# A turn of products by column lanes and the neighbouring full turn, multiplied column block by column block

## The chip, the core and the metric

The kernel runs on one core of a Trainium2 chip. The metric is the device time of one execution in microseconds. TensorE multiplies, VectorE (DVE), ScalarE (ACT) and GpSimd (POOL) compute beside it, SyncE (SP), ACT and POOL issue DMAs, and 16 DMA engines move the data.

## The reference

One layer of an encoder on 256 positions of width 2048: modulated norms, a conv group and an attention group, an output projection, and then a retrieval over 16384 experts (`peer_ffn`). The change lies in the last sum of that retrieval. For each token, 8 heads choose 16 experts each; cut to what matters:

```python
expert = i1 * 128 + i2                       # 8 heads x 16 experts a token
a   = einsum('td,tnd->tn', h, u_tab[ids])    # u_tab: 16384 x 2048
act = gelu(a) * gate
out = einsum('tn,tnd->td', act, v_tab[ids])  # v_tab: 16384 x 2048
y   = rms_norm(x + gt_f * out, g_final)
```

## The kernel before, in words

The retrieval is dense in its first half: for each of the 128 blocks of 128 experts, `ru` (1 MB of `peer_u`) is loaded, split in a high and a low part (L239, L240), and multiplied with the tokens (`pu`, lines 257 to 263). Gate times GELU of these scores, zero where a token did not choose the expert, is written to memory (`actd`, one row of 256 tokens per expert).

The second half is sorted. While the scores are still made, POOL sorts the experts by which of eight groups of 32 tokens use them, so that they fill 109 blocks of 128 experts (`ORDER` is their order). A block needs, for each half `tt` of 128 tokens, all four groups, or a pair of neighbouring ones, or a single one. `plan()` turns this, as plain Python while the program is built, into a list of 89 **turns**:

- 48 *full* turns: one block, one half of the tokens, 128 columns of weights;
- 21 *pair* turns: two blocks side by side, each with 64 columns;
- 20 *single* turns: four blocks side by side, each with 32 columns.

In pairs and singles the blocks sit in column lanes of TensorE (`tile_position`), and their matmuls go at the same time. The list mixes the kinds as blocks come up; the last four turns are full ones (`DEFER`).

For a block, POOL gathers 128 rows of `peer_v` (L1355, `fetch_raw`, 128x2048 in float32, into a tile named `rv`, `rvd`, `rvg`, `early` or `A`) and the matching rows of `actd` (L1366, `fetch_m`, into `mc` or `mcs`). A lane multiplies these two as they are, in float32; each such product is two weight loads and two matmuls in the records. A full turn uses parts: `split_to` (L246 on ACT, L247 on DVE) makes high and low parts of the rows (`hwhi`/`hwlo`, the two halves of `hboth`, and near the end `hx`) and of the weights (`mhl`), and three products are summed, high by high, low by high, high by low. The parts have three slots to begin with (`wide`); up to 15 blocks are fetched ahead (`AHEAD`).

`product` (L1444) is one product of one column block: 512 of the 2048 columns of the result (`d4` from 0 to 3). The eight tiles `po` (two halves of tokens by four column blocks) hold the sum in PSUM through the whole stage. TensorE runs the products in the order in which they are written (`keep`); gathers, splits and products wait for each other by semaphores.

The loop that writes them goes over the turns with index `i`. Ahead of each group of turns it frees slots and tiles of turns below `i`, writes the gathers and splits that are due, and then the products:

```python
for d4s in ((range(4),) if len(group) == 1 and group[0][0][2] == "full" else [(d4,) for d4 in range(4)]):
    for k, p in enumerate(group):
        for t in range(3):
            for n, at, kind in p:
                if t == 0 or kind == "full":
                    r, m = split[n][t] if kind == "full" else (raws[n], ms[n])
                    for d4 in d4s:
                        product(r, m, at, SIZE[kind], d4, ...)
i += len(group)
```

So a full turn by itself takes its three products in turn, each through the four column blocks. A turn by lanes goes by column block, with all its lanes in each. Before the change a group is one turn, but for the last three turns, which are one group and go by column block. When the products are done, `finish` scales the sum, adds it to `x`, normalises and writes the result.

Of the kernel before, what the change touches and what calls it, by code (L numbers as in the profile page):

```python
# [10 lines left out]
F32R = mybir.dt.float32r  # L11
# [156 lines left out]
def hybrid_block_kernel(  # L168
# [25 lines left out]
    cst = ctx.enter_context(tc.tile_pool(name="cst", bufs=1))  # L194
# [93 lines left out]
    with tc.tile_pool(name="pre", bufs=1) as pre:  # L288
# [482 lines left out]
        for q in range(4):  # L771
# [4 lines left out]
            for u in range(4 * NG0):  # L776
                g, n = divmod(u, 4)
                i = NG0 * q + g
# [567 lines left out]
    turns, need = plan()  # L1346
# [104 lines left out]
        for _ in range(4 * (1 - k)):  # L1451
            fetch_m(m_free.pop(0)[-1])
    wide = [(-1, [wp.tile([128, 2048], F32R, tag=t, name=f"h{t}{k}") for t in ("whi", "wlo")]) for k in range(2)]
    both = cst.tile([128, 2, 2048], F32R, tag="T1", name="hboth")
    wide.append((-1, [both[:, 0], both[:, 1]]))
    mhl = cst.tile([128, 8, 256], F32R, tag="T3a", name="mhl")
    narrow = [(-1, k) for k in range(4)]
    mcs = cst.tile([128, 8, 256], F32, tag="T3b", name="mcs")
# [40 lines left out]
    first_last = len(turns) - len(DEFER)  # L1499

    i = 0
    while i < len(turns):
        group = turns[i:i + 1] if i < len(turns) - 3 else turns[i:]
        now = max(x[0] for p in group for x in p)
        for x in [x for x in live if x[0] < i]:
            live.remove(x)
# [194 lines left out]
```

## Time and profile before

| what | value |
|---|---|
| median of three runs | 1691.31 us (1676.72 to 1833.54) |
| the profiled execution | 1675.07 us, span 1673.3 us |
| mean granted TensorE clock | 0.980 |
| first matmuls of `po` in the trace | about 1321 us |
| first turn by lanes | 1334 us |
| last matmul of `po` | ends about 1660 us |
| DMA over the whole span | 502.55 MB, mean 300 GB/s |

Times in the trace are microseconds from the start of the span. A row of the timeline has the start, the length from the first start to the last end, the engine (PE is TensorE's matmuls, PEld its weight loads), the line, the operation, result and operands, the shapes (rows*columns of weights, then the moving operand), the count, and in brackets the idle time ahead of it with what ended it. A row of waits has who waited, for whom, the total in us, how often, and the longest.

### The profile page before, as it was taken

Reading aid. Unit: us, or ns where it says so; the run is one execution under the profiler, and the core shown is the slowest. Engines: PE = TensorE matmul, PEld = TensorE weight load, DVE = VectorE, ACT = ScalarE, POOL = GpSimd, SP = SyncE. Lnnn points to the kernel's source line nnn. Section 1 sums busy time; section 2 is a strip of 40 time slices with the busy share of each in tenths; the row PEclk is TensorE's granted clock in tenths of the full one; section 3 lists DMA queues with packets and bytes.
Section 4 is the critical chain, followed back from the end, with each engine's and each line's share of the span. In section 5 each row is a group of like instructions: output and inputs, shape, how many; then the busy total and the mean of one; then the engine's idle time right before and its main releaser. Section 6 shows DMA issues by size and latency. Waiting matters only on the chain.

```text
span 1673.3 us, 30110 instructions
## 1 busy us (share of the span) xinstructions
PE 1595.5 (95%) x12776; PEld 1387.4 (83%) x12780; DVE 1124.2 (67%) x1610; ACT 707.6 (42%) x901; POOL 430.4 (26%) x356
## 2 busy tenths in 40 slices
PE   3999999999999999999999999999999989899996
PEld 2879899999899999999999999999999746433443
DVE  5778778867678889998997875575765425222316
ACT  3225557544544446655663334343343324222213
POOL 0000000000000000000000007888873466565651
PEclk9999999999999999999999999999999999999998
DMA  9996998889665556656668789999999889999995
GB/s 395 425 410 233 351 337 328 310 303 335 239 233 172 187 203 202 243 175 239 224 235 285 249 272 270 302 363 361 335 348 397 299 347 346 360 379 375 378 345 226
DMA packets 115725, 502.55 MB, mean 300 GB/s; under 512 B 13392, under 2 KB 55888, under 8 KB 60288
## 3 DMA queue, kind: packets, MB, share of 16 engines
q1 hardware_dynamic: 44640, 319.79, 51.6%
q0 software_dynamic: 25184, 129.25, 20.2%
q10 hardware_dynamic: 45760, 51.51, 9.6%
q8 instruction: 102, 1.67, 0.4%
q14 instruction: 39, 0.32, 0.1%
HBM read 462.57 MB, written 37.94 MB: 299 GB/s over the span
## 4 chain that ended last, share of the span: by engine, by line
PE 84%; DVE 7%; issue 4%; DMA 3%; ACT 1%; SPq 0%; DVEq 0%; ACTq 0%
PE po L1444 19%; PE pu L257 11%; PE pu L258 11%; PE pu L263 11%; PE pin L748 4%; DMA ru<-in_peer_u_dram 3%; PE pwin L257 2%; PE pwin L258 2%; PE pwin L263 2%; DVE lu L240 2%; PE pwout L257 2%; PE pwout L258 2%; PE pwout L263 2%; PE pq L258 2%; PE pq L257 2%
## 5 line engine op out<-in xcount | busy, mean ns | idle before, releaser
L257 PE MATMUL pu<-h2hi,hu 128*128 128x256 f32 x2048 | 481.0, 280 | 2.8 <-ACT hu L239 2.8
L239 ACT ACTIVATE hu<-ru 128x2048 fp32r<-128x2048 f32 x128 | 245.8, 1920 | 393.7 <-PE pu L258 286.2
L240 DVE TENSOR_TENSOR lu<-ru,hu 128x2048 fp32r<-128x2048 f32 x128 | 293.1, 2290 | 167.3 <-ACT hu L239 125.4
L257 PEld LDWEIGHTS pu<-h2hi,hu 128*128 128x128 f32 x2048 | 385.8, 188 | 3.6 <-ACT hu L239 3.2
L263 PE MATMUL pu<-h2hi,lu 128*128 128x256 f32 x2048 | 253.9, 276 | 0.9 <-DVE lu L240 0.9
L258 PE MATMUL pu<-h2loT3b,hu 128*128 128x256 f32 x1024 | 247.5, 278 | 0.0
L1288 POOL DMA_INDIRECT permd<-work x126 | 206.6, 1639 | 148.8 <-DVE work L1284 110.7
L263 PEld LDWEIGHTS pu<-h2hi,lu 128*128 128x128 f32 x2048 | 242.0, 188 | 1.1 <-DVE lu L240 1.1
L258 PE MATMUL pu<-h2loT3a,hu 128*128 128x256 f32 x1024 | 241.2, 278 | 0.0
L1320 POOL DMA_DIRECT2D gg<-gd x3 | 4.2, 1398 | 882.1 <-DMA permd<-pad 882.1
L258 PEld LDWEIGHTS pu<-h2loT3b,hu 128*128 128x128 f32 x1024 | 192.9, 188 | 0.2 <-issue 0.2
L258 PEld LDWEIGHTS pu<-h2loT3a,hu 128*128 128x128 f32 x1024 | 193.0, 188 | 0.0
L1444 PE MATMUL po<-rv,mc 128*32 128x512 f32 (+1 forms) x336 | 94.5, 601 | 3.1 <-issue 2.6
L1355 POOL DMA_INDIRECT rv<-in_peer_v_dram,perm_idx x66 | 67.9, 1029 | 96.3 <-ACT A L1386 29.9
L1444 PE MATMUL po<-hwhi,mhl 128*128 128x512 f32 x272 | 79.5, 413 | 12.2 <-issue 12.1
L240 DVE TENSOR_TENSOR lwin<-rwin,hwin 128x2048 fp32r<-128x2048 f32 x33 | 75.5, 2289 | 21.7 <-ACT hwin L239 20.3
L239 ACT ACTIVATE hwin<-rwin 128x2048 fp32r<-128x2048 f32 x33 | 63.1, 1912 | 57.2 <-PE pin L748 31.8
L1444 PE MATMUL po<-rv,mcs 128*32 128x512 f32 (+1 forms) x312 | 86.2, 628 | 1.0 <-issue 0.7
L1444 PEld LDWEIGHTS po<-hwhi,mhl 128*128 128x128 f32 x272 | 51.7, 195 | 38.0 <-issue 25.5
L257 PE MATMUL pwin<-hhi,hwin 128*128 128x256 f32 x336 | 81.0, 285 | 0.0
L258 PE MATMUL pwin<-hlo,hwin 128*128 128x256 f32 x336 | 78.7, 278 | 0.0
L284 DVE SCALAR_TENSOR_TENSOR acc<-ada,cact,acc 128x2048 f32<-128x2048 f32 x30 | 70.4, 2347 | 10.1 <-DMA ada<-in_w_ada_dram 9.7
(594 smaller groups left out, 3173.5 us busy)
## 6 DMA issues: line engine op xcount, KB each, us to landing
ru<-in_peer_u_dram SPq DMA_DIRECT2D x128, 1024.0 KB
ada<-in_w_ada_dram SPq DMA_DIRECT2D x96, 1024.0 KB
rwin<-in_w_in_dram SPq DMA_DIRECT2D x33, 1024.0 KB
rwout<-in_w_out_dram SPq DMA_DIRECT2D x16, 1024.0 KB
rwq<-in_w_q_dram SPq DMA_DIRECT2D x16, 1024.0 KB
gd<-stage ACTq DMA_DIRECT2D x16, 1024.0 KB
actd<-A ACTq DMA_DIRECT2D x14, 1024.0 KB
gg<-gd ACTq DMA_DIRECT2D x13, 1024.0 KB
```

Of the source, the lines that this page charges most:

```text
L239: S.activation(hi, raw, AF.Copy)
L240: lo_op = V.tensor_tensor(lo, raw, hi.bitcast(F32), ALU.subtract)
L257: PE.matmul(dst, lhsT=whi[:, sl], rhs=rhi[:, c], start=(c == sets[0][0]), stop=False)
L258: PE.matmul(dst, lhsT=whi[:, sl], rhs=rlo[:, c], start=False, stop=False)
L263: PE.matmul(dst, lhsT=wlo[:, sl], rhs=rhi[:, c], start=False, stop=(c == cs[-1] and cs == last))
L284: op = V.scalar_tensor_tensor(acc, raw, cact[:, k:k + 1], acc, ALU.mult, ALU.add)
L748: PE.matmul(dst, lhsT=wt[:, (4 * n + j) * 128:(4 * n + j + 1) * 128], rhs=ht[:, 4 * q + j], start=start, stop=stop, skip_group_check=True)
L1288: put_one = nc.gpsimd.indirect_dma_start(permd[:, :], bass.IndirectOffsetOnAxis(ap=place[:, i:i + 1], axis=0), ids[:, i:i + 1], None)
L1320: keep((S if 1 < k < NG - 1 else nc.gpsimd).dma_start(gg, gd[:, :, k * ABLK:(k + 1) * ABLK, :].rearrange("tb p i t -> p tb i t")))
L1355: keep(nc.gpsimd.indirect_dma_start(raw, None, v_rows, index(ORDER[len(raws)])))
L1444: keep(PE.matmul(po[tt * 4 + d4][row:row + size], lhsT=m[:, at * size:(at + 1) * size], rhs=raw[:, d4 * 512:(d4 + 1) * 512], start=start, ...
```

## The change

Where exactly one of two neighbouring turns is full, and both lie ahead of the last four turns (`first_last`), they now form one group. A group of two goes by column block: for each of the four, the first turn's products and then the second's. A tile's Python name is changed as well, since `both` is now that condition.

```diff
-    both = cst.tile([128, 2, 2048], F32R, tag="T1", name="hboth")
-    wide.append((-1, [both[:, 0], both[:, 1]]))
+    hboth = cst.tile([128, 2, 2048], F32R, tag="T1", name="hboth")
+    wide.append((-1, [hboth[:, 0], hboth[:, 1]]))
...
     while i < len(turns):
-        group = turns[i:i + 1] if i < len(turns) - 3 else turns[i:]
+        both = i + 1 < first_last and (turns[i][0][2] == "full") != (turns[i + 1][0][2] == "full")
+        group = turns[i:i + 1 + both] if i < len(turns) - 3 else turns[i:]
```

The list of turns gives 28 such groups: 10 of a full turn and a pair, 4 of a pair and a full turn, 7 of a full turn and singles, 7 of singles and a full turn. On TensorE, between matmuls of L1444 next to each other in the program, 22 go from 128 columns to fewer and 22 back before the change, and 106 each way after it; 9 go between 64 and 32 columns in both.

TensorE where the first full turn and the first pair meet, before (`hboth` are the parts of the full turn's block; `po` 14769 to 14772 are the four column blocks of the first half of the tokens, 14773 to 14776 those of the second):

```order
L1444 MATMUL po_14769<-hboth,mhl 128x512
L1444 MATMUL po_14770<-hboth,mhl 128x512
L1444 MATMUL po_14771<-hboth,mhl 128x512
L1444 MATMUL po_14772<-hboth,mhl 128x512
L1444 MATMUL po_14773<-rv_13991,mc_14648 64x512
L1444 MATMUL po_14773<-early,mc_14647 64x512
L1444 MATMUL po_14774<-rv_13991,mc_14648 64x512
L1444 MATMUL po_14774<-early,mc_14647 64x512
```

These are the last four of the full turn's twelve rows and the first four of the pair's eight. The same place after the change, the whole of both turns:

```order
L1444 MATMUL po_14769<-hboth,mhl 128x512 x3
L1444 MATMUL po_14773<-rv_13991,mc_14648 64x512
L1444 MATMUL po_14773<-early,mc_14647 64x512
L1444 MATMUL po_14770<-hboth,mhl 128x512 x3
L1444 MATMUL po_14774<-rv_13991,mc_14648 64x512
L1444 MATMUL po_14774<-early,mc_14647 64x512
L1444 MATMUL po_14771<-hboth,mhl 128x512 x3
L1444 MATMUL po_14775<-rv_13991,mc_14648 64x512
L1444 MATMUL po_14775<-early,mc_14647 64x512
L1444 MATMUL po_14772<-hboth,mhl 128x512 x3
L1444 MATMUL po_14776<-rv_13991,mc_14648 64x512
L1444 MATMUL po_14776<-early,mc_14647 64x512
```

The full turn's three products of a column block now stand together, and the pair's of the same block behind them; the kind of matmul changes seven times where it changed once.

TensorE a little later, where four singles and the next full turn meet, before, from the singles' last column block on:

```order
L1444 MATMUL po_14772<-early,mc_14647 32x512
L1444 MATMUL po_14772<-rv_14110,mc_14648 32x512
L1444 MATMUL po_14772<-rv_14224,mc_14649 32x512
L1444 MATMUL po_14776<-early,mc_14647 32x512
L1444 MATMUL po_14769<-hwhi_14789,mhl 128x512
L1444 MATMUL po_14770<-hwhi_14789,mhl 128x512
L1444 MATMUL po_14771<-hwhi_14789,mhl 128x512
L1444 MATMUL po_14772<-hwhi_14789,mhl 128x512
```

And after, from the singles' first column block on:

```order
L1444 MATMUL po_14769<-early,mc_14647 32x512
L1444 MATMUL po_14769<-rv_14110,mc_14648 32x512
L1444 MATMUL po_14769<-rv_14224,mc_14649 32x512
L1444 MATMUL po_14773<-early,mc_14647 32x512
L1444 MATMUL po_14769<-hwhi_14789,mhl 128x512
L1444 MATMUL po_14769<-hwlo_14790,mhl 128x512
L1444 MATMUL po_14769<-hwhi_14789,mhl 128x512
L1444 MATMUL po_14770<-early,mc_14647 32x512
L1444 MATMUL po_14770<-rv_14110,mc_14648 32x512
L1444 MATMUL po_14770<-rv_14224,mc_14649 32x512
L1444 MATMUL po_14774<-early,mc_14647 32x512
```

Here the full turn's first matmul moves from behind all sixteen products of the singles to behind four of them, and the singles' last products move behind three quarters of the full turn.

POOL has the same 109 gathers by L1355 in both programs, block by block in the same order; which tile a block lands in differs, since groups give their tiles back two turns at a time. A stretch of its queue before:

```order
L1366 DMA mc_14647<-actd,ident 128x128
L1355 DMA early<-in_peer_v_dram,perm_idx 128x2048
L1366 DMA mcs<-actd,ident 128x128
L1355 DMA rvd_14779<-in_peer_v_dram,perm_idx 128x2048
L1366 DMA mcs<-actd,ident 128x128
L1355 DMA rv_14110<-in_peer_v_dram,perm_idx 128x2048
```

And the same stretch after:

```order
L1366 DMA mcs<-actd,ident 128x128
L1355 DMA early<-in_peer_v_dram,perm_idx 128x2048
L1366 DMA mc_14647<-actd,ident 128x128
L1355 DMA rv_14110<-in_peer_v_dram,perm_idx 128x2048
L1366 DMA mc_14648<-actd,ident 128x128
L1355 DMA rv_14224<-in_peer_v_dram,perm_idx 128x2048
```

The gathers are the same blocks in the same order; `rvd` and `mcs`, which stood here before, are taken by other blocks now. ACT and DVE have as many instructions as before; a few splits stand some places apart, and read other tiles.

## The prediction

> **What bounds the kernel now.** I read the page's head and its chain first, then the windows of the last stage, who waits there, and last the timeline of TensorE.
>
> ```profile
> PE 1595.5 (95%) x12776; PEld 1387.4 (83%) x12780; DVE 1124.2 (67%) x1610; ACT 707.6 (42%) x901; POOL 430.4 (26%) x356
> PE 84%; DVE 7%; issue 4%; DMA 3%; ACT 1%; SPq 0%; DVEq 0%; ACTq 0%
> ```
>
> ```profile
> 1334.00:1660.00 326.00, 303.45 (x1529) 151.50 (x1528) 106.24 (x195) 88.95 (x186) 187.66 (x194) 0.95 0.90 353
> 1407.00:1445.00 38.00, 38.00 (x197) 22.66 (x194) 13.50 (x24) 11.62 (x24) 25.15 (x25) 1.00 0.91 349
> 1572.00:1583.00 11.00, 11.00 (x49) 7.34 (x49) 2.87 (x5) 2.50 (x5) 8.49 (x9) 1.00 1.01 408
> ```
>
> From the page's head (busy time, share of the span, instructions) and its chain line: TensorE carries the chain of work that ended last. The window rows (length; busy time of PE, PEld, DVE, ACT, POOL; granted clock; DMA share; GB/s) say the same of the last stage: from the first turn by lanes, at 1334, to the last matmul, at 1660, TensorE is busy for 303 of 326 us. DMA is the close second: 0.90 of the stretch, 353 GB/s.
>
> Who waits for whom between 1334 and 1648:
>
> ```profile
> PEld po L1444 <- issue: 146.8, 344, 2.6
> PEld po L1444 <- DMA A<-in_peer_v_dram,perm_idx: 0.9, 1, 0.9
> PEld po L1444 <- ACT mhl L246: 1.7, 2, 0.8
> POOL rv L1355 <- PE po L1444: 21.7, 15, 4.0
> POOL rv L1355 <- DVE hwlo L247: 16.7, 3, 6.5
> ```
>
> TensorE's waits for gathered rows or for a split are about 1 us each. POOL, which issues the gathers, waits for TensorE's buffers and for the splits, and those wait for TensorE's slots. So gathers run ahead of the products, and the order of products sets the stage. "Issue" is time that no releaser explains.
>
> The price of the products, from turns that run undisturbed. A turn by four lanes of 32 columns, two full turns, and the next lanes:
>
> ```profile
> 1391.00 0.59 PE L1444 MATMUL po<-rvd,mcs 128*32 128x512 f32 x1
> ...
> 1391.43 0.59 PE L1444 MATMUL po<-rvd,mcs 128*32 128x512 f32 x1
> ...
> 1391.97 3.03 PE L1444 MATMUL po<-hboth,mhl 128*128 128x512 f32 x12
> 1394.84 1.10 PE L1444 MATMUL po<-hwhi,mhl 128*128 128x512 f32 x4
> 1395.78 1.07 PE L1444 MATMUL po<-hwlo,mhl 128*128 128x512 f32 x4
> 1396.69 1.08 PE L1444 MATMUL po<-hwhi,mhl 128*128 128x512 f32 x4
> ...
> 1397.71 0.62 PE L1444 MATMUL po<-rvd,mcs 128*32 128x512 f32 x1
> ...
> 1398.16 0.59 PE L1444 MATMUL po<-rvd,mcs 128*32 128x512 f32 x1
> ...
> 1398.59 0.59 PE L1444 MATMUL po<-rvd,mcs 128*32 128x512 f32 x1
> ```
>
> Starts are what counts, since matmuls overlap. One lane's matmuls start every 0.43 us (1391.00, 1391.43). All lanes go side by side, and each product is two records, so a lane turn is 8 such waves, 8 x 0.43 = 3.44 us. Full matmuls start every 0.23 (eight from 1394.84 to 1396.69: 1.85), so a full turn of 12 is 2.76.
>
> A change of kind costs extra. Lanes to full: 0.54 from the last wave to the first full matmul (+0.11), and the first twelve take 2.87 for 2.76 (+0.11). Full to lanes: four take 1.01-1.02 for 0.92 (+0.09), and the first wave lasts 0.45 for 0.43 (+0.02). There and back is 0.33 to 0.34. With lanes of 64 columns ("pair"):
>
> ```profile
> 1498.55 0.59 PE L1444 MATMUL po<-early,mc 128*64 128x512 f32 x1
> ...
> 1498.98 0.59 PE L1444 MATMUL po<-early,mc 128*64 128x512 f32 x1
> ...
> 1499.51 3.02 PE L1444 MATMUL po<-hboth,mhl 128*128 128x512 f32 x12
> 1502.36 1.10 PE L1444 MATMUL po<-hwhi,mhl 128*128 128x512 f32 x4
> ...
> 1504.21 1.08 PE L1444 MATMUL po<-hwhi,mhl 128*128 128x512 f32 x4
> 1505.22 0.64 PE L1444 MATMUL po<-rv,mc 128*64 128x512 f32 x1
> ...
> 1505.70 0.59 PE L1444 MATMUL po<-rv,mc 128*64 128x512 f32 x1
> ```
>
> 0.10 + 0.09 + 0.09 + 0.05 = 0.33. I take **0.34 us per round**, both kinds.
>
> The stage's work from 1334 on: 46 full turns x 2.76 = 127, 41 lane turns x 3.44 = 141, 22 rounds x 0.34 = 7.5, and about 1 for nine changes between the lane widths: 277 of the 326 us. The missing **49 us** are slow stretches:
>
> ```profile
> 1334.02 0.64 PE L1444 MATMUL po<-rv,mc 128*64 128x512 f32 x1
> ...
> 1338.88 1.32 PE L1444 MATMUL po<-rv,mc 128*64 128x512 f32 x2 [1.53 <-issue]
> 1341.69 1.01 PE L1444 MATMUL po<-early,mc 128*64 128x512 f32 x1 [1.50 <-issue]
> 1343.09 1.01 PE L1444 MATMUL po<-early,mc 128*64 128x512 f32 x1 [0.39 <-issue]
> 1344.49 1.01 PE L1444 MATMUL po<-early,mc 128*32 128x512 f32 x1 [0.39 <-issue]
> ...
> 1351.04 1.18 PE L1444 MATMUL po<-hwhi,mhl 128*128 128x512 f32 x4
> ```
>
> ```profile
> 1336.80:1346.00 9.20, 4.84 (x8) 0.82 (x6) 0.00 (x0) 1.14 (x3) 5.00 (x6) 0.76 1.01 419
> 1445.40:1453.80 8.40, 3.35 (x8) 1.65 (x8) 0.15 (x1) 0.81 (x2) 4.46 (x5) 0.82 1.00 407
> ```
>
> Starts lie 1.4 us apart, and nothing shown releases them: these two lane turns, 1334.02 to 1351.04, take 17.0 us for 2 x 3.44 and the changes, 7.3, so 10 are lost here alone. In these stretches DMA is full, at over 400 GB/s; but it is full from 1572 to 1583 too, with TensorE undisturbed. Full DMA goes with them and is not enough to cause one. Why they come the trace doesn't show.
>
> **The change part by part.** Of 89 turns, 28 neighbours of different kinds become a group (14 with singles, 14 with pairs). A group goes through four column blocks, and each holds the lanes' two waves and three full matmuls.
>
> *Products.* Their number and shapes stay: nothing saved. Three full matmuls now follow each other into one bank, where before neighbours went to four banks. The last three turns do that already:
>
> ```profile
> 1652.98 0.86 PE L1444 MATMUL po<-hx,mhl 128*128 128x512 f32 x3
> 1653.68 0.86 PE L1444 MATMUL po<-hboth,mhl 128*128 128x512 f32 x3
> ```
>
> Three in 0.70, 0.23 each: free.
>
> *Changes of kind.* A group had one change inside; it now has seven, so six more, three rounds. 28 x 3 = 84 rounds more, at 0.34: **+29 us** (bounds 28 to 30 by the two fences). All of it is TensorE's own time in the stage that it bounds; nothing lies beside it to hide it, unless the stage is held by something else at the same moment, and that is the 49 us.
>
> Could a change inside a group be cheaper than one between turns, since its loads wait for no new data?
>
> ```profile
> 1391.97 0.99 PEld L1444 LDWEIGHTS po<-hboth,mhl 128*128 128x128 f32 x5 [0.84 <-issue]
> 1457.85 1.12 PEld L1444 LDWEIGHTS po<-hboth,mhl 128*128 128x128 f32 x5
> 1458.08 1.31 PE L1444 MATMUL po<-hboth,mhl 128*128 128x512 f32 x5
> ```
>
> From full to full the load starts 0.23 ahead of its matmul (1457.85, 1458.08), though it opens a new turn. After lanes it starts with the matmul (1391.97), with the load path idle for 0.84 before. So it is the kind that holds the load back, and I take the full price. The Trainium skill's page "TensorE: Matmul & The Clock Gate", Part 3, The mechanism, says otherwise: weight loads are pulled ahead of matmuls in flight when they go to another row group or to the background weights. By that rule the loads inside a group would hide; the second rival gives the time that this makes. The trace at 1391.97 doesn't bear it out across a change of kind.
>
> *Buffers.* A lane's gathered rows are read in the last column block, so in a group that starts with lanes they come free some 3 us later (the full turn's 2.76 plus the changes); in one that starts with the full turn the lanes are read earlier and also end last. The POOL queue behind such a gather waits as long, and after it the splits. Against this stands TensorE's small wait for data, 1 us at a time, so this costs 0 (bounds 0 to 5: once 0.9 to 1.7 us for two or three releases). The splits' slots free by column block, earlier than now: nobody on the path waits for that.
>
> *Slow stretches.* At 408 GB/s (the full row above) the 115 MB of the stretch (353 x 326) take 282 us. TensorE's work is 277 now, so it demands a little more than DMA can give, and DMA fills up. With the change it is 306, 24 more than DMA needs: POOL gets its buffers later, and queues drain. POOL adds no burst of its own, as one gather takes it 1.25 us:
>
> ```profile
> 1329.53 0.94 POOL L1366 DMA_INDIRECT mcs<-actd,perm_idx  x1 [0.30 <-issue]
> 1330.78 0.95 POOL L1355 DMA_INDIRECT rvd<-in_peer_v_dram,perm_idx  x1 [0.30 <-issue]
> ```
>
> A block takes POOL two gathers, 2.5 us, and DMA 2.8: rows of 128 x 2048 x 4 bytes and weights of 64 or 128 KB are 1.15 MB, at 408 GB/s. A backlog grows by 0.3 us per block, only while POOL runs on without a wait. Bounds: all 49 us stay and grow with the stage (+5), or all go (-49). I take **-20**: the first stretch, with its 10 us, follows the entry into the stage, which the change hardly touches, and of the other 39 half goes, for want of a row that says more.
>
> *Everything ahead of 1331* is as it was, and so are the final turns and the end.
>
> Sum: the profiled execution took 1675.07 (span 1673.3, 1.8 around it). 1675 + 29 - 20 = **1684 us**. The median of the three runs shown is 1691.31, the quickest 1676.72, so this execution stands with the quickest. Between kernels about 2%, 34 us, is what a measurement tells from no change.
>
> **The rivals.**
>
> 1. *The slow stretches are TensorE's own and stay.* Mechanism: they come per time spent in the stage, whatever DMA does. Place: turns by lanes and full turns alike, as now. Price: 49 x 306/277 = 54, so +29 + 5 = +34, 1709. For it: DMA is full in clean stretches too. Against: the two stretches shown lie where DMA is full. From the point that the stretches lose under 1 us the kernel is slower by 2%: this is the other side. With them just unchanged it is 1704.
> 2. *Loads inside a group are pulled ahead.* Then a round keeps the 0.09 to 0.11 of the gaps and loses the exposed loads, 0.11 and 0.02 to 0.05: 84 x 0.14 = 12 less, +17, and 1672 with the same -20. Against it speaks 1391.97.
> 3. *The stretches vanish.* DMA no longer fills up, and 49 - 5 go: 1675 + 29 - 44 = 1660. For it: the 24 us of room. Against: releases still come in clumps, now two turns at once.
> 4. *Nothing is gained or lost*, because DMA is the true limit and the new time only fills what TensorE lost: +29 - 29, 1675. Against: POOL waits for TensorE's buffers, not the other way round.
>
> **How the numbers follow.** Forecast (stretches lose 10 to 30 us, 1674 to 1694): 0.48. Rival 1, 1700 to 1718: 0.22, of it 0.12 over the 2% mark at 1709. Rival 2: 0.08. Rival 3: 0.12. Rival 4: 0.10. The range for 8 in 10 runs from 1660, the full gain, to 1712, the full price and a little of a growing remainder. Faster by over 2% would need 1642, below rival 3 and 2 together with all stretches gone (1648): 0.03, for what none of these names; as much on the other side makes slower 0.15. The same: 0.82.
>
> **What would show it.** In the changed trace: TensorE's changes between 128 and 32 or 64 columns rise by 168, each way at the prices above; a group lasts 7.5 us instead of 6.5; the load after lanes starts with its matmul. DMA's share from 1334 on falls below 0.90, POOL's waits for TensorE grow, and starts 0.7 or 1.4 us apart with "issue" become fewer. The last matmul ends about 9 us later. I'm wrong if a round inside a group has another price, if TensorE begins to wait for gathers or splits by more than 5 us in all, or if the slow stretches answer to something else than DMA's backlog.

## The result, and the profile after

The changed kernel is a little slower. On the chip of the first comparison its median is 1692.89 us (21 executions), that of the kernel before 1683.94 (21 executions); the ratio is 1.0079, 95% interval 1.0052 to 1.0106. The medians count every execution, while the ratio leaves out the slow ones, among them two of before and four of the changed kernel that took 1827 to 1848 us. By the bound of 2% the ratio counts as no change; by its own interval it is a loss of 9 to 18 us, 13 in the middle. The profiled execution took 1684.22 us with a span of 1682.4, against 1675.07 and 1673.3.

The page's head and chain line of the changed kernel:

```profile
PE 1609.3 (96%) x12776; PEld 1368.5 (81%) x12780; DVE 1126.1 (67%) x1610; ACT 711.1 (42%) x901; POOL 433.7 (26%) x356
PE 80%; DVE 7%; issue 5%; DMA 3%; POOL 2%; ACT 2%; another core or an unknown queue 0%; SPq 0%; DVEq 0%; ACTq 0%; POOLq 0%
```

Its window from 1334 to 1660 (length; busy time of PE, PEld, DVE, ACT, POOL; granted clock; DMA share; GB/s):

```profile
1334.00:1660.00 326.00, 310.17 (x1488) 127.11 (x1487) 99.20 (x175) 85.54 (x170) 191.52 (x194) 0.97 0.91 351
```

And who waits between 1334 and 1648:

```profile
PEld po L1444 <- issue: 166.7, 302, 2.0
POOL rv L1355 <- PE po L1444: 18.9, 11, 3.4
PEld po L1444 <- ACT hwhi L246: 7.4, 9, 0.8
POOL rvd L1355 <- PE po L1444: 7.2, 3, 4.8
POOL early L1355 <- PE po L1444: 5.1, 3, 3.0
POOL rvg L1355 <- PE po L1444: 2.7, 2, 1.4
PEld po L1444 <- ACT mhl L246: 1.7, 2, 0.8
PE po L1444 <- DMA rv<-in_peer_v_dram,perm_idx: 1.0, 1, 1.0
```

Nothing new holds TensorE: no wait for a gather or a split is over 1.0 us. Weight loads wait for these more often, 11.9 us in all instead of 5.4, but that is time ahead of the load and need not stop the matmuls. The span is 9.1 us longer, and it is all in the last stage, where the last matmul starts at 1668.66 instead of 1659.71. In the timeline of TensorE, two column blocks of a group of singles with a full turn:

```profile
1390.90 0.62 PE L1444 MATMUL po<-rvd,mcs 128*32 128x512 f32 x1
...
1391.35 0.59 PE L1444 MATMUL po<-rvd,mcs 128*32 128x512 f32 x1
...
1391.89 0.50 PE L1444 MATMUL po<-hwhi,mhl 128*128 128x512 f32 x1
1392.23 0.39 PE L1444 MATMUL po<-hwlo,mhl 128*128 128x512 f32 x1
1392.47 0.40 PE L1444 MATMUL po<-hwhi,mhl 128*128 128x512 f32 x1
1392.79 0.62 PE L1444 MATMUL po<-rvd,mcs 128*32 128x512 f32 x1
...
1393.25 0.59 PE L1444 MATMUL po<-rvd,mcs 128*32 128x512 f32 x1
...
1393.79 3.06 PE L1444 MATMUL po<-hboth,mhl 128*128 128x512 f32 x12
```

One column block takes 1.89 us from lanes to lanes (1390.90 to 1392.79): 0.45 and 0.54 for the two waves, 0.34, 0.24 and 0.32 for the three full matmuls. Bare work is 2 x 0.43 + 3 x 0.23 = 1.55, so the round costs 0.34.

Below, a kernel's *stage* is the time from the start of the first matmul of `po` to the start of the last, read from its trace. (In the profile of before the first one starts at 1316.08, not at about 1321.) Its work, with no slow stretch and no wait, is 294.8 us for the order before; how that is found stands with the experiments. What the stage takes beyond its work is called *lost*. In this first pair the stage went from 343.6 to 353.9 us; 28.8 of work came, and the loss fell from 48.8 to 30.3. The stage also began 1.3 us earlier, which makes its 10.2 us into the 8.95 of the last matmul.

### The profile page after: what moved, and what is told of

Read it like the earlier page. It is cut to its first block, busy times and chain, and to the rows that moved or that the text cites. A ratio compares the mean times of both kernels' runs of the same rounds, so it can differ in the third digit from the quotient of the medians.

```text
span 1682.4 us, 30108 instructions
## 1 busy us (share of the span) xinstructions
PE 1609.3 (96%) x12776; PEld 1368.5 (81%) x12780; DVE 1126.1 (67%) x1610; ACT 711.1 (42%) x901; POOL 433.7 (26%) x356
## 3 DMA queue, kind: packets, MB, share of 16 engines
q0 software_dynamic: 25184, 129.25, 20.2%
## 4 chain that ended last, share of the span: by engine, by line
PE 80%; DVE 7%; issue 5%; DMA 3%; POOL 2%; ACT 2%; another core or an unknown queue 0%; SPq 0%; DVEq 0%; ACTq 0%; POOLq 0%
PE po L1444 15%; PE pu L257 11%; PE pu L258 11%; PE pu L263 11%; PE pin L748 4%; PE pwin L257 2%; PE pwin L258 2%; PE pwin L263 2%; DVE lu L240 2%; PE pwout L257 2%; PE pwout L258 2%; PE pwout L263 2%; PE pq L258 2%; PE pq L257 2%; PE pq L263 2%
## 5 line engine op out<-in xcount | busy, mean ns | idle before, releaser
L1444 PE MATMUL po<-rv,mc 128*32 128x512 f32 (+1 forms) x336 | 111.5, 610 | 2.3 <-issue 2.2
L1444 PEld LDWEIGHTS po<-hwhi,mhl 128*128 128x128 f32 x272 | 51.8, 192 | 73.8 <-issue 58.9
L1444 PE MATMUL po<-hwhi,mhl 128*128 128x512 f32 x272 | 102.4, 432 | 4.0 <-issue 3.0
L1444 PE MATMUL po<-rv,mcs 128*32 128x512 f32 (+1 forms) x288 | 92.0, 603 | 0.0
L1355 POOL DMA_INDIRECT rv<-in_peer_v_dram,perm_idx x67 | 67.1, 1001 | 82.8 <-DMA actd<-A 28.2
L239 ACT ACTIVATE hwin<-rwin 128x2048 fp32r<-128x2048 f32 x33 | 63.1, 1913 | 57.1 <-PE pwin L258 21.7
```

The lines of the kernel that those rows point to most:

```text
L239: S.activation(hi, raw, AF.Copy)
L1355: keep(nc.gpsimd.indirect_dma_start(raw, None, v_rows, index(ORDER[len(raws)])))
L1444: keep(PE.matmul(po[tt * 4 + d4][row:row + size], lhsT=m[:, at * size:(at + 1) * size], rhs=raw[:, d4 * 512:(d4 + 1) * 512], start=start, ...
```

## Experiments

The chips differ. On the chips numbered 5, 15 and 2 the kernel before has a median of 1655.80, 1653.79 and 1656.53 us, on those numbered 11 and 10 it has 1684.16 and 1685.19, as on the first. The slow stretches were seen on the latter kind alone. Ratios are to the kernel before, measured beside it on the same chip; the stage and the loss are those of one profiled execution of each kernel.

| kernel | chip | rounds or matmuls added | stage, us | lost, us | ratio (95%) |
|---|---|---|---|---|---|
| before, first pair | | 0 | 343.6 | 48.8 | |
| after, first pair | | 84 rounds | 353.9 | 30.3 | 1.0079 (1.0052 to 1.0106) |
| early_before | 11 | 0 | 339.5 | 44.7 | 0.9984 (0.9952 to 1.0015) |
| singles_only | 11 | 42 rounds | 346.1 | 36.9 | 1.0055 (1.0005 to 1.0106) |
| pairs_only | 11 | 42 rounds | 345.7 | 36.5 | 1.0012 (0.9966 to 1.0058) |
| early_after | 11 | 84 rounds | 354.1 | 30.5 | 1.0074 (1.0034 to 1.0113) |
| half_before_c | 10 | 0 | 342.7 | 47.9 | 1.0049 (1.0010 to 1.0089) |
| padded_c | 10 | 112 full matmuls | 351.4 | 31.8 | 1.0077 (1.0031 to 1.0124) |
| before_again | 15 | 0 | 305.8 | 11.0 | |
| blocks_alone | 15 | 0 | 306.0 | 11.2 | 1.0032 (0.9992 to 1.0071) |
| padded | 15 | 112 full matmuls | 319.6 | 0 | 1.0118 (1.0065 to 1.0171) |
| after_again | 15 | 84 rounds | 323.6 | 0 | 1.0102 (1.0062 to 1.0141) |
| whole | 5 | 0 | 310.9 | 16.1 | 1.0007 (0.9968 to 1.0046) |
| two_blocks | 5 | 28 rounds | 304.4 | 0 | 1.0017 (0.9978 to 1.0055) |
| half_before, half_before_b | 5, 2 | 0 | 302.4, 297.3 | 7.6, 2.5 | 0.9923 (0.9879 to 0.9968), 0.9922 (0.9881 to 0.9964) |
| half_after, half_after_b | 5, 2 | 84 rounds | 323.6, 323.6 | 0, 0 | 1.0066 (1.0027 to 1.0105), 1.0078 (1.0033 to 1.0122) |
| padded_b | 2 | 112 full matmuls | 319.6 | 0 | 1.0029 (0.9985 to 1.0073) |
| ahead9 | 2 | 0 | 315.6 | 20.8 | 1.0036 (0.9995 to 1.0077) |

### The price of a round

The grouping alone, and a third of the rounds. Both kernels take the changed kernel's groups; `whole` multiplies each turn of a group whole, `two_blocks` goes through a group by two column blocks at a time:

```diff
-        for d4s in (... [(d4,) for d4 in range(4)]):            # the change: a group of two by one block
+        for d4s in (... [range(4)] ...):                        # whole
+        for d4s in (... [(0, 1), (2, 3)] if len(group) == 2 ...):  # two_blocks
```

> The changed kernel's groups of two turns, with their gathers, splits and tiles written where the changed kernel writes them, but in each group the first turn's products stand whole ahead of the second's: no rounds added. Theory (only the rounds cost): within 4 us of before. Rival (tiles and slots given back two turns at a time, and gathers into other tiles, carry part of the change): slower by 5 to 13 us, 0.3 to 0.8%, with waits of TensorE for gathers or splits.

> The changed kernel's groups, taken through two halves of two column blocks each instead of four single ones: one added round a group, 28 in all. Theory: 28 x 0.34 = 9.5 us more of TensorE's work, of which the slow stretches give back a part as in the changed kernel (there 20 of 29): 2 to 6 us slower than before, so hard to tell from it, and the trace shows the changes of kind at the same prices. Rival (the grouping costs, not the rounds): as slow as the changed kernel, 9 to 13 us.

A stage without an idle slot gives the price of a round. In these three window rows TensorE is busy from end to end. `two_blocks`:

```profile
1350.00:1636.90 286.90, 286.90 (x1531) 139.70 (x1528) 104.53 (x188) 88.25 (x181) 191.45 (x194) 1.00 0.98 401
```

The changed kernel on chip 15 (after_again):

```profile
1334.00:1642.00 308.00, 308.00 (x1539) 130.93 (x1537) 109.96 (x197) 93.28 (x188) 193.33 (x196) 1.00 0.94 376
```

The changed order with half rows (half_after_b, next section):

```profile
1349.00:1656.00 307.00, 307.00 (x1534) 130.44 (x1535) 111.73 (x199) 94.31 (x189) 192.88 (x196) 1.00 0.68 209
```

Stages of 304.4 us with 28 rounds and 323.6 with 84: (323.6 - 304.4) / 56 = **0.343 us per round**. Without rounds that leaves 323.6 - 84 x 0.343 = 294.8, the work of the order before; the prediction's own count, 277 from the first lanes on and 17.9 ahead of them, is 294.9. It can be read directly, too. Up to the 1451st of the 1592 matmuls of `po` the order before takes 269.07 us on chip 15 (before_again), with no wait on the way; the rest takes 25.07 in half_before_b. The sum, 294.1, is 0.7 less, and makes the round 0.35.

In `whole` the 1451st matmul starts after the same 269.07 us, so grouping by itself, with its later buffers, costs TensorE nothing. Only behind it is more time lost to late data than in before_again, on another chip (16.1 us against 11.0). The interval of its ratio is that of 5 us less to 8 us more.

One bank after another. Every full turn by itself goes by column block, in the order of before:

```diff
-        for d4s in ((range(4),) if len(group) == 1 and group[0][0][2] == "full" else [(d4,) for d4 in range(4)]):
+        for d4s in [(d4,) for d4 in range(4)]:
```

> The order of before with every full turn by itself multiplied column block by column block, three matmuls into one bank behind each other, and no round added. The step 'three full matmuls into one bank are free': ratio 0.998 to 1.002. Rival, a bank pays for its own successor: at 0.02 us per matmul, 46 x 12 x 0.02 = 11 us, 1.007; at 0.05 it would be 28 us, 1.017, and the 29 us would have been that.

306.0 us against 305.8, and 269.07 us to the 1451st matmul in both, ahead of the waits at the end that could hide a price: three full matmuls into one bank cost nothing.

Both widths of lanes. Only the groups with lanes of 32, or only those with lanes of 64, go by column block:

```diff
+ [range(4)] if len(group) == 2 and min(SIZE[p[0][2]] for p in group) != 32 else ...   # singles_only; != 64 for pairs_only
```

> The changed kernel's groups, but only the 14 groups with lanes of 32 columns go column block by column block; in the 14 with lanes of 64 each turn is multiplied whole. 42 rounds instead of 84: 14.3 us more of TensorE's work. Theory 1: the last stage before has a slack of some 11 us on the chips seen so far without slow stretches (305.8 us from the first to the last matmul of the stage, of which 294.9 are work), which the first rounds use up, and the rest counts in full: 294.9 + 14.3 = 309 us, 3 to 4 us over before, ratio 1.000 to 1.004. Rival, each round costs its share of the measured 15 us: 305.8 + 7.5 = 313, ratio 1.0045.

> The same with only the 14 groups with lanes of 64 columns mixed. Theory 1: 42 rounds of 0.33 to 0.34, 308 to 309 us in the stage, ratio 1.000 to 1.004. Rival: 313 us, 1.0045. If the two widths don't have one price, the two kernels' stages differ by more than 2 us.

346.1 and 345.7: one price. The absolute numbers expected were for the other kind of chip; these two ran on one with slow stretches, and the loss of 36.9 and 36.5 lies between those without rounds (44.7) and with 84 (30.5).

### Where part of the 29 us goes on a chip without slow stretches

Both kernels once more, with a profile of each from one chip:

> The kernel before, for a profile on the same chip as the other kernels of this call. Theory 1: from the first lane turn to the last matmul it takes 277 us plus its slow stretches and half-clock windows, and 20 to 31 us less than the changed kernel in the same stretch where both show none. Theory 2: both take 282 to 300 us there, DMA's time at 400 GB/s, with TensorE waiting for gathered rows by tens of us.

> The changed kernel once more, beside the kernel before, on whatever chip this is. Theory 1: the 84 rounds cost TensorE 29 us plus 0 for the buffers, and what came back in the first profiled pair (19 us) came from two things that differ by chip and execution: stretches in which TensorE gets one instruction every 0.70 us, and windows of half the granted clock that follow a pause of TensorE. On a chip that shows few of them the ratio is then 1.012 to 1.018 (20 to 29 us of some 1655); on one that shows them as the first did, 1.005 to 1.010. Theory 2: DMA is the true limit of the last stage at over 400 GB/s and swallows the rounds; then the ratio is 1.000 to 1.004 where DMA is full and TensorE waits for it.

The kernel before on chip 15 (before_again), its stage by windows:

```profile
1352.00:1450.00 98.00, 98.00 (x538) 59.16 (x537) 40.47 (x72) 34.63 (x70) 72.48 (x74) 1.00 1.01 410
1450.00:1550.00 100.00, 100.00 (x553) 48.04 (x551) 30.70 (x56) 27.59 (x58) 69.95 (x72) 1.00 1.01 417
1550.00:1600.00 50.00, 50.00 (x287) 21.39 (x288) 10.94 (x20) 8.60 (x19) 33.95 (x36) 1.00 1.01 416
1600.00:1640.00 40.00, 32.66 (x156) 15.76 (x156) 21.40 (x41) 16.12 (x35) 11.33 (x12) 0.96 0.74 303
```

And what its matmuls waited for there (us in total, times, longest):

```profile
PE po L1444 <- DMA mcs<-actd,ident: 2.8, 1, 2.8
PE po L1444 <- ACT mhl L246: 1.9, 2, 1.2
PE po L1444 <- DMA mc<-actd,perm_idx: 1.4, 1, 1.4
```

DMA is full for 250 us at 410 to 417 GB/s, with TensorE undisturbed, and the lead of the gathers is used up at 1600: the last blocks come late, TensorE waits, its clock drops once, and 11 us are lost. The changed kernel asks for less per us, and in its row above nothing is lost. Its stage is 17.8 us longer than that of before_again, 28.8 of work less 11.0. Another 2.3 us come back behind the last matmul (16.0 us before, 13.7 after), where in before DVE is still at the first half of the tokens. The medians say much the same: 1668.37 less 1653.79, 14.6 us. (The two profiled executions have one span, 1655.7 and 1655.6, since the stage of before_again begins 15.6 us later, behind the load `gg` below.)

Half rows take that cover away: half of each row is gathered from the tenth block on and used twice.

```diff
...
-        keep(nc.gpsimd.indirect_dma_start(raw, None, v_rows, index(ORDER[len(raws)])))
+        keep(nc.gpsimd.indirect_dma_start(raw[:, :1024], None, peer_v.rearrange("b p (h d) -> (b p h) d", h=2), rows))
...
```

> The order of before; from the tenth block on a gather fetches only half of each expert's row (4 KB instead of 8 KB), and the products and splits of the other two column blocks read that half again. So the output is another one; TensorE's instructions and their order are as before, and DMA moves about half as much in the last stage. Theory (the slow stretches come with a backlog of gathers in DMA): they go nearly all, the stage from the first turn by lanes to the last matmul falls from 326 us to 277 to 285, and the kernel is 40 to 49 us faster than before, ratio 0.970 to 0.976. Rival (the stretches are TensorE's own): 49 us of starts 0.7 or 1.4 us apart stay, and the time is that of before within 5 us.

> The order of the changed kernel, with the same half rows (output another one, TensorE's instructions those of the changed kernel). Theory: no slow stretches here either, so the whole price of the 84 added rounds shows: 28 to 30 us above the half-row kernel in the old order, which makes about 1655 us or 0.985 to 0.992 of before, though the change with full rows cost only 9 to 13 us. Rival (the stretches are TensorE's own and the mixed order itself cures some): the difference between the two half-row kernels is again 9 to 13 us.

The first pair ran on a chip without slow stretches, so what was expected of these wasn't tested, and both ratios missed. It gave 302.4 and 323.6, 21.3 us apart, and medians 22.2 apart; 4.2 of the missing 7.6 us in half_before were one wait for a split (`hwhi`). It was measured again:

> The order of before, with half of each row gathered from the tenth block on and used twice (the output differs), for a chip with slow stretches. Theory 1, the stretches need a full DMA: with a DMA share of some 0.7 they vanish, the stage loses under 10 us instead of 45 to 49, and the ratio is 0.976 to 0.982 there; on a chip without stretches 0.990 to 0.996. Rival, they belong to TensorE on that chip whatever DMA does: the stage still loses over 30 us, ratio 0.99 to 1.00.

> The changed order with half rows. Theory 1: nothing left to give back but some 5 us of waits, so 21 to 29 us above half_before_b on any chip, and with slow stretches elsewhere the ratio to before with full rows is 0.990 to 1.000. Rival: the stretches stay and shrink as before, and it is 10 to 15 us above half_before_b.

With DMA at 0.74 the order before loses 2.5 us, and the changed order is 26.3 us longer in the stage and 29.1 in the median (1668.89 and 1639.79). The rounds' price shows nearly whole. So on such a chip some 11 of 29 us are DMA's: rival 4, in part.

Earlier waits had to be kept apart from this. On these chips one load ahead of the stage (`gg`) often lands late (46.2 us after its request in before_again, where DVE waited 18.4 us for it), and executions of most kernels fall into two groups 10 to 15 us apart. A kernel pair with this load asked for three blocks earlier:

```diff
-        asks.setdefault(at - (6 if 1 < k < NG - 1 else 3), []).append(k)
+        asks.setdefault(at - (9 if k == NG - 2 else 6 if 1 < k < NG - 1 else 3), []).append(k)
```

> The kernel before with one load moved: the last but one of the gate weights (gg) is asked for nine blocks ahead instead of six. On the last two chips it landed 46 us after its request, behind the first gathers, DVE and TensorE waited, and executions fell into two groups some 13 us apart. Theory: landing ahead of the gathers removes the slower group: median 11 us lower at most, ratio 0.990 to 0.996. Rival: DMA's queue is full whatever goes first, and another transfer is late instead: 0.998 to 1.002.

> The changed kernel with the same load moved. Theory 1 (84 rounds at 0.34, the last stage's slack of 11 us, the rest in full): 14 to 18 us above early_before, whatever the move itself does; ratio 1.000 to 1.006 against the kernel before if it helps as hoped. Rival, DMA is the limit of both: within 5 us of early_before.

They ran on chip 11, where the profiles of singles_only and pairs_only show no such wait without the move, so the profiles don't test it, and by its ratio, 0.9984, early_before is no change. Yet its twelve executions all took 1671 to 1682 us, while 18 of the 35 of the kernel before took 1683 to 1699; whether the move removed those stays open. What the pair does give is the change's effect once more, 1677.58 to 1691.06, 13.5 us, with stages of 339.5 and 354.1.

### What the slow stretches are

Theory of the prediction: DMA's backlog, and the change gives it room. Two readings of the trace before speak against it. The first is the granted clock, two windows from within one stretch:

```profile
1473.50:1478.00 4.50, 1.52 (x4) 0.60 (x4) 1.79 (x4) 1.42 (x5) 2.95 (x3) 1.00 1.01 412
1478.10:1484.80 6.70, 5.68 (x13) 1.76 (x15) 5.37 (x10) 4.04 (x9) 4.34 (x4) 0.50 0.93 352
```

The second is the timeline of TensorE's loads and matmuls over the same time:

```profile
1473.54 0.19 PEld L1444 LDWEIGHTS po<-hwhi,mhl 128*128 128x128 f32 x1
...
1474.16 0.40 PE L1444 MATMUL po<-hwhi,mhl 128*128 128x512 f32 x1 [0.23 <-issue]
1474.86 0.19 PEld L1444 LDWEIGHTS po<-hwhi,mhl 128*128 128x128 f32 x1 [1.13 <-issue]
...
1475.59 0.39 PE L1444 MATMUL po<-hwhi,mhl 128*128 128x512 f32 x1 [1.03 <-issue]
...
1477.00 0.19 PEld L1444 LDWEIGHTS po<-hwhi,mhl 128*128 128x128 f32 x1 [1.95 <-issue]
...
1477.70 0.40 PE L1444 MATMUL po<-hwhi,mhl 128*128 128x512 f32 x1 [1.73 <-issue]
...
1480.55 1.06 PE L1444 MATMUL po<-rvd,mcs 128*64 128x512 f32 x1
...
1481.40 1.06 PE L1444 MATMUL po<-rvd,mcs 128*64 128x512 f32 x1
```

A stretch has two parts. First TensorE begins one instruction every 0.70 us, load or matmul alike (0.62, 0.70, 0.73, 1.41, 0.70), at the full granted clock. Some 4.5 us later the granted clock falls to 0.50 for 6.8 us, and waves of lanes that came every 0.43 come every 0.85. The Trainium skill's page "TensorE: Matmul & The Clock Gate", Part 1, What's actually happening, states that the clock passes half its pulses after an idle window of about 3.4 us; the trace agrees in the length, since its half-clock windows are 3.4 us long or a multiple, but what goes ahead of them here is a spell of little work, not an idle one (TensorE busy for 1.52 of 4.50 us). By the clock records of the trace the stage of before has five of 6.8 us, at half rate some 17 us of the loss; after has 17 us of them, some 8.5. So 8.5 of the 18.5 us that came back are half-clock time.

The stretches aren't scattered. In each of the eight profiles that show them, whatever the order, one begins 1 to 9 us after the first turn by lanes and one 225 to 239 us after it. What ties them to these places the traces don't show.

Whether the stretches need DMA, and whether they answer to added changes of kind or to added time, was tried with half rows and with a kernel that repeats the first product of the 28 full turns in question, 112 full matmuls:

```diff
-                for t in range(3):
+                for t in ((0, 0, 1, 2) if i in beside and p[0][2] == "full" else range(3)):
```

> The order of before, but each of the 28 full turns that the change puts beside lanes repeats its first product, four full matmuls: 112 x 0.23 = 25.8 us more of TensorE's work, with no change of kind added; the output is then another. Theory 1, TensorE's added time counts whatever it is made of: the same per us as the rounds, so a ratio within 0.003 of 0.9 times the changed kernel's distance from 1 in this call (1.011 to 1.016 without slow stretches). Rival, it is the mixing of kinds that costs or that quiets the slow stretches: padded then differs from the changed kernel by more than 10 us, with the changes of kind dearer than 0.34 where it is the quicker one.

> The order of before with 112 repeated full matmuls, 25.8 us of TensorE's time and no change of kind added. Theory, any added time of TensorE gives DMA room: on a chip with slow stretches they lose 13 to 19 us, the ratio is 1.004 to 1.009, as the changed kernel's. Rival, only the changes of kind quiet them: they stay at 45 to 49 us, the ratio is 1.014 to 1.018.

> 112 repeated full matmuls, 25.8 us, on such a chip. Theory: the stretches lose 13 to 19 us of their 45 to 49, ratio 1.004 to 1.009. Rival, only the changes of kind quiet them: ratio 1.014 to 1.018. Without stretches 1.003 to 1.012 as twice measured, the stage at 319.6 us.

> Half rows with the order of before, for a chip that shows slow stretches (before at some 1684). Theory 1, they need a full DMA: they vanish, the stage loses under 10 us, ratio 0.976 to 0.982. Rival, they are that chip's whatever DMA does: over 30 us lost, ratio 0.99 to 1.00. On a chip without them 0.990 to 0.993 as twice measured, and the question stays open.

Without slow stretches padded takes 319.6 us twice, 294.8 + 112 x 0.22, nothing lost; its ratios, 1.0118 and 1.0029, spread, presumably by the two groups of executions, and take the changed kernel's 1.0102 between them. On chip 10 the half-row kernel, two windows in a stretch and the whole stage:

```profile
1339.30:1343.40 4.10, 1.20 (x5) 0.21 (x2) 0.00 (x0) 1.26 (x2) 3.19 (x4) 1.00 0.81 250
1343.60:1353.70 10.10, 7.41 (x20) 1.82 (x23) 4.21 (x8) 3.70 (x7) 3.77 (x4) 0.50 0.51 167
1334.00:1660.00 326.00, 307.31 (x1534) 156.16 (x1533) 109.03 (x199) 92.26 (x188) 188.73 (x196) 0.96 0.63 197
```

DMA has 0.63 of the stage and 197 GB/s, and the loss is 47.9 us, as with full rows on the other chips that show stretches (48.8, 44.7). **The theory of the backlog falls**: a full DMA is not needed. On the chips without stretches DMA was full (413 GB/s) and none came. Half rows don't make the gathers fewer, though (25184 packets on their queue in both), so a part of their number isn't excluded; and the ratio, 1.0049, lies above every range expected, which the profile doesn't explain.

padded_c, with no round added, has a loss of 31.8 instead of some 47, as the changed kernel has 30.3 and 30.5. So the stretches shrink with added TensorE time of either kind. That is one profiled execution, the quickest of seven; over its executions the ratio says that 13 of the 24.8 us showed (5 to 21). By rounds the loss goes 48.8 and 44.7 (none), 36.9 and 36.5 (42), 30.3 and 30.5 (84): 16 us less for 28.8 us of work.

One more try at the backlog, gathers asked for at most 9 blocks ahead (`AHEAD = 9` for 14):

> The kernel before with gathers asked for at most 9 blocks ahead instead of 14, so that fewer stand in DMA's queues. If a backlog in the queues makes the slow stretches, they shrink by 10 us or more on a chip that has them, unless the shorter lead makes TensorE wait for rows by as much: ratio 0.985 to 0.995. If the backlog doesn't matter: 0.998 to 1.005.

It ran on chip 2, with no stretches to shrink. The shorter lead makes the late data worse (weight loads; the matmuls' own waits for `mhl` are 13.6 us):

```profile
PEld po L1444 <- ACT mhl L246: 18.6, 8, 7.9
```

20.8 us lost instead of about 11, ratio 1.0036. What makes TensorE begin only one instruction in 0.70 us on some chips, and why added time makes it rarer, stays open. The runs exclude that the stretches need a full DMA, and that only changes of kind shrink them; the number of gathers no run changed.

## Why the prediction was right or wrong

**The sum came close, in part by luck, and it was set on the wrong base.** It said 1675 + 29 - 20, so 9 us more; the profiled executions differ by 9.15 us (1675.07, 1684.22), the medians of 21 by 8.95, and the ratio says 13 (9 to 18), so that +9 lies at its near edge. The step that failed is the last sentence of the sum: the profiled execution stood with the quickest, and the forecast of 1684 was given in its place against a median of 1691.31, so that it read as a gain of 7, where the runs showed a loss of 0.8%. The median of more executions before is 1683.94, and 9 on top is the 1692.89 measured. A second step failed in its reason: the -20 was put down to DMA's queues, and by the prediction's own last sign of being wrong the stretches answer to something else.

- *Changes of kind, +29.* Right: 84 rounds at 0.343, from stages without any wait.
- *Three full matmuls into one bank, 0.* Right (blocks_alone).
- *Buffers, 0.* Right: `whole` and before_again keep one time to the 1451st matmul, and after_again, whose buffers are those of the change, loses nothing.
- *Slow stretches, -20.* The size was close (-18.5 in the first pair, -14.2 on chip 11), but half of 39 had been taken for want of a row that says more, so this is luck, and the reason was wrong. "Nothing shown releases them" overlooked the clock column of the rows that stood beside it, 0.76 and 0.82. "Queues drain" is refuted by half_before_c; why added work shrinks the stretches stays open. That the first stretch stays was right: 11.5 us before, 11.4 after.
- *Rival 1, the stretches are TensorE's own and stay.* Its first half holds so far as they don't need a full DMA; its second doesn't, they shrink by about a third.
- *Rival 2, loads pulled ahead.* Refuted: a round inside a group costs what one between turns does, 0.34. After lanes the first full matmul and its successor are 0.34 apart (1391.89 to 1392.23), the exposed load.
- *Rival 3, the stretches vanish.* Not on that chip.
- *Rival 4, DMA is the limit.* In part, and elsewhere: on chip 15 DMA's late data hid 11 of the 29 us. POOL waiting for TensorE's buffers, the argument against it, did not exclude it: the gathers' lead can still run out at the end of the stage.
- *Signs.* The last matmul came 8.95 us later, as said. A group of singles lasts 4 x 1.89 = 7.6, as said. Starts held back by "issue" became fewer (30 on TensorE's matmuls before, 18 after). POOL's waits for TensorE grew as said, from 28.1 us (21.7 for `rv`, 4.5 for `rvd`, 1.9 for `A`) to 33.9 in the four rows above, though those for `rv` alone fell. DMA's share, 0.90 before, is 0.91 up to 1660 and 0.89 up to the last matmul, so it hardly fell. The waits of weight loads for gathers and splits grew by 6.5 us, more than the 5 that the prediction allowed, but without effect: in after_again those for `hwhi` alone are 13.1 us, with TensorE busy from end to end.

## What to carry to other kernels

A switch between column lanes and the full array has a price, here 0.34 us there and back, so turns of one kind belong together. Mixing them finer is paid nearly in full where TensorE works without a break (26.3 of 28.8 us with half rows), and in part where the stage loses time otherwise, to late data or slow stretches. Read the granted clock of a slow stretch before blaming the engine that looks full, and test the blame by taking half of its load away. Put a forecast on the base that it will be compared with: a difference worked out on one quick execution goes on top of the median, not on that execution.

## What the runs showed of the hardware

- Chips of one type differ by 1.7% on this kernel (medians of about 1655 and 1684 us), mostly by stretches in which TensorE begins one instruction per 0.70 us at the full granted clock, with DMA at 0.63 as well as full.
- A pause of TensorE, or a slow spell of some 4.5 us such as those with 1.52 of 4.50 or 1.20 of 4.10 us busy, was followed by 3.4, 6.8 or more us at half the granted clock, so a wait can cost more than its length. On chip 15 the clock fell 2.6 us into the wait for a late split ahead of the stage (no matmul starts from 1291.1 to 1302.0), and stayed there to its end:

```profile
1291.10:1294.00 2.90, 0.19 (x2) 0.00 (x0) 0.00 (x0) 0.00 (x0) 0.00 (x0) 0.98 1.04 320
1294.00:1302.00 8.00, 0.00 (x0) 0.00 (x0) 4.54 (x3) 0.00 (x0) 1.98 (x1) 0.50 0.23 92
```

- Added work of TensorE can fill time that is otherwise lost to late data: 28 rounds, 9.6 us of work, moved the time by a ratio of 1.0017 (0.9978 to 1.0055), with a stage of 304.4 us against 305.8 of before_again, whose DMA is full and which loses 11.0 us; the next 56 lengthen the stage by 19.2 us.
